# Rotation of the keys two products earlier in an in-order schedule (hybrid attention and gMLP block, one core)

## The chip, the cores and the metric

One NeuronCore of a Trainium2 chip runs the whole program. The metric is the device time of one execution in microseconds; the kernel before takes 1201.62 us (median of three runs, 1200.4 to 1201.99).

## The reference: what is computed

The block has 2048 tokens of width 1024. An RMS norm with a shift and a scale that come from a vector c gives h; one wide product gives all branches; attention (window of 128, 8 query heads, 2 key heads, a learned sink in each softmax) and a gated MLP that mixes over tokens in chunks of 128 are gated, projected, merged and projected again. What bears on the change is the rotation of q and k by the token's position:

```python
h = _rms(x, g_pre[l]) * (1.0 + scale) + shift
proj = h @ w_in[l]
q, k, v, z_a, u_b, v_b, z_b, g_logits = jnp.split(proj, SPLIT_IDX, axis=-1)
q = _rope(q.reshape(b, s, N_Q_HEADS, HEAD_DIM), positions)
k = _rope(k.reshape(b, s, N_KV_HEADS, HEAD_DIM), positions)

def _rope(t, positions):
    half = HEAD_DIM // 2
    inv_freq = ROPE_THETA ** (-jnp.arange(half, dtype=jnp.float32) / half)
    ang = positions.astype(jnp.float32)[..., None] * inv_freq
    cos = jnp.cos(ang)[:, :, None, :]
    sin = jnp.sin(ang)[:, :, None, :]
    t1, t2 = tf[..., :half], tf[..., half:]
    return concatenate([t1 * cos - t2 * sin, t2 * cos + t1 * sin], axis=-1)
```

## The kernel before, in words

**Tiles and products.** Tokens are handled in two halves of 1024 (`s` = 0, 1). The wide product is cut into 19 column groups of 256; each group is a 2 by 2 block product that is done with seven block products (numbered p = 0 to 6) instead of eight. One such product is 12 matmuls of 128x128 by 128x512: four slices of the inner dimension, three matmuls each, since every fp32 operand is split into a high and a low part (`mm3`, line 170). I call these "products" and number them as the program does with `slot`, from 0, along the first token half. The groups are: two of the MLP's v branch, the keys and values (`ev_kv`, line 983), one of gates, the first half of the queries (`ev_q`, line 1015), and so on. The first four groups are run side by side, so that products 0 to 27 belong to them, in turn: the key group's quarter for tokens 0 to 511 (call it k0) comes out of product 14, its quarter for tokens 512 to 1023 (k1) out of product 22. From product 28 on the groups follow one another, seven products each: 28 to 34 are the first queries, 35 to 41 a gate group, 42 to 48 the other queries.

**An order written out by hand.** Every engine executes its instructions strictly in the order in which the program issues them. Side work is hung on products: `later(n, f)` puts f ahead of the product n places on; with `True` behind it, with `"mid"` in its middle (after two of the four inner slices). Hooks of one place run in the order in which they were registered. An instruction hung on product 33 is therefore not at the time of product 33: it comes when its engine has done all that was issued earlier. This holds for the DMA queue of SyncE (SP) too: all loads and stores named here are issued by SP, in this order, and a transfer whose source isn't ready holds up all behind it.

**Weights.** `w_get` ahead of product n prepares the weight of product n + 3: SP loads `raw`, GpSimd (POOL) forms a sum of quarters where needed, ScalarE (ACT) casts the high part (line 223), and VectorE (DVE) subtracts for the low part ahead of the next product (lines 158 and 224). There are four weight buffers, so the cast for product n + 3 waits until product n - 1 is done.

**The rotation.** `rope_out` (line 639) turns the angles into a sine and a cosine table on ACT and stores both to DRAM (`cs`). `load_rope` (line 861) loads from there four tables, sine and cosine for each 512 tokens (`ropet`, buffers `m`), each by four DMAs of 64 KB; three products after a sine table's load ACT flips the sign of half its rows (line 870). `rope_finish` (line 947) has five steps, at 1, 5, 6, 8 and 9 products plus `wait` after the quarter came out: `turn` loads the quarter (`R`) and a copy with rows exchanged in pairs (two DMAs); `mix` multiplies the copy by the sine on POOL (line 961) and `R` by the cosine on DVE (line 962); `both` adds them on DVE and casts the high part on ACT; `low` subtracts on DVE; `put_out` stores high and low part (`k_s`). In the first token half the raw keys are kept in DRAM (`kr`) until then, so that a `turn` for them is three DMAs.

**What lies around it.** Ahead of or behind the same products hang: `setup_sgu` (product 26: loads of `wT` and `Tt`), `zero_heads` (28), `ln_step` (line 920) of the MLP branch, whose first three loads `q<-vb` (line 923) hang on products 27, 29 and 32, and whose transposes on TensorE (line 929) come behind products 31, 33 and 36 and wait for those loads; `h1_stats` (line 1189; product 30, then each fifth), which loads a row block of x and squares it on ACT three products on. A quarter that comes out of product p = 4 of a group is finished by an addition on DVE, `add(c, b["Y"], self.wsb)` (lines 436 and 164), and product p = 6 of that group, which accumulates in the same bank Y, waits until DVE has read it. In the gate group of products 35 to 41 these are product 39 and product 41.

Of the kernel before, what the change touches and what calls it, by code (L numbers as in the profile page):

```python
# [55 lines left out]
def hybrid_block(ctx: ExitStack, tc: tile.TileContext, xt, x, wada, wgate, wI, wP, wO,  # L56
# [30 lines left out]
    def flat(tag, dt=F32):  # L87
        return t2(tag, [P, 512], dt)
# [10 lines left out]
    def dram(name, shape):  # L99
        return tc.dram_tile(shape, F32, name=name)  # L100
# [16 lines left out]
    kr_s = [dram(f"kr{i}", [P, TG]) for i in range(2)]  # L117
# [39 lines left out]
    def sub(o, a, b):  # L157
        dve.tensor_tensor(out=o, in0=a, in1=b, op=ALU.subtract)  # L158

    def psub(o, a, b, op=ALU.subtract):  # L160
        pool.tensor_tensor(out=o, in0=a, in1=b, op=op)  # L161

    def add(o, a, b):
        dve.tensor_tensor(out=o, in0=a, in1=b, op=ALU.add)  # L164
# [64 lines left out]
    def later(n, f, post=False):  # L229
        hooks.setdefault((slot[0] + n, post), []).append(f)  # L230
# [630 lines left out]
    def load_rope(s, ns):  # L861

        def one(h, i, key):
            g = 2 * s + h
            t = flat("m")
            for r in range(4):
                at = 64 * (r // 2) + r % 2
                sp.dma_start(t[at : at + 64 : 2, :] if at < 64 else t[at:P:2, :], cs_s[i][32 * g : 32 * (g + 1), :])
            if key == "s":
                later(3, lambda: act.activation(out=t, in_=t, func=AF.Copy, scale=col[:, C_SGN : C_SGN + 1]))  # L870
            ropet[key, h] = t
        for h in range(2):
            for i, key in enumerate("cs"):
                later(ns[2 * h + i], lambda h=h, i=i, key=key: one(h, i, key))
# [29 lines left out]
    def half(key):  # L904
        return int(key[1]) - 1

    def ft(key):
        return int(key[0]) - 1

    def store(n, dst, t):  # L910
        later(n, lambda: sp.dma_start(dst, t))
# [35 lines left out]
    def rope_finish(h, R, put_out, wait, raw=None):  # L947
        st = {}

        def turn():  # L950
            nonlocal R
            if raw is not None:
                R = flat("x")
                sp.dma_start(R, raw)
            st["hi"] = flat("x", F32R)
            st["rot"] = st["hi"].bitcast(F32)
            for r in range(2):
                sp.dma_start(st["rot"][r:P:2, :], (R if raw is None else raw)[1 - r : P : 2, :])

        def mix():  # L960
            psub(st["rot"], st["rot"], ropet["s", h], ALU.mult)
            dve.tensor_tensor(out=R, in0=R, in1=ropet["c", h], op=ALU.mult)

        def both():
            add(R, R, st["rot"])
            act.copy(st["hi"], R)

        def low():
            sub(R, R, st["rot"])
        later(1 + wait, turn)  # L970
        later(5 + wait, mix)
        later(6 + wait, both, True)
        later(8 + wait, low)
        later(9 + wait, lambda: put_out(st["rot"], R))

    def rope_in(src, psum, tag):
        if not psum:
            return src
        R = flat(tag)
        act.copy(R, src)  # L980
        return R

    def ev_kv(s):
        def ev(key, src, psum):
            h = half(key)
            if ft(key) == 0:
                def put_out(hi, lo):
                    ks = slice(P + s * NT + h * 512, P + s * NT + (h + 1) * 512)
                    for i, t in enumerate((hi, lo)):
                        sp.dma_start(k_s[:, i, ks], t)  # L990
                R = rope_in(src, psum, "e")
                if s == 0:
                    store(1, kr_s[h], R)
                rope_finish(h, R, put_out, (15, 9)[h] if s == 0 else h, kr_s[h] if s == 0 else None)
            else:
                t = src
                if psum:
                    t = flat("e")
                    act.copy(t, src)

                def turn():
                    b = bank()
                    for c in range(4):
                        pe.transpose(b[:, c * P : (c + 1) * P], t[:, c * P : (c + 1) * P], ident)

                    def out_():
                        o = flat("qS"[s])
                        act.copy(o, b)
                        at = 1 + s * 8 + h * 4
                        store(1, v_s[:, at : at + 4, :], o.rearrange("p (a b) -> p a b", a=4))  # L1010
                    later(1, out_)
                later((3, 10)[h] if s == 0 else 2, turn, True)
        return ev
# [309 lines left out]
    def run_all():  # L1323
        nonlocal T

        for s in range(NS):
# [6 lines left out]
            if s == 0:  # L1333
                later(26, setup_sgu)
                later(28, zero_heads)
            load_rope(s, ((29, 28, 31, 30), (10, 11, 12, 13))[s])
            for i in range(8):
                later((27 + 5 * i // 2, 17 + 3 * i)[s], lambda i=i: ln_step(s, i))
            for c in range(4):
# [25 lines left out]
            if s == 0:  # L1365
                n0 = NFIRST
                S = pS.tile([P, 2, 512], F32, tag="s", name=nm("s"))
                bX = bank()
                rows["bank"] = bank()
                bks = [two_banks(BK["X"], BK["W"]), two_banks(BK["Y"], BK["Z"]), two_banks(S[:, 0, :], S[:, 1, :]),  # L1370
                       two_banks(bX, rows["bank"])]
                blks = [Block(bks[i], kinds[i](), "mmee"[i]) for i in range(NFIRST)]

                def second_root():
                    sum_to(NFIRST + 1)
                    rstd(1, BK["Z"])

                def second_half():
                    ada_row(1, range(0, 1))
                    want(NFIRST)  # L1380
                    want(NFIRST + 1)
                    sum_to(NFIRST + 3)
                    low_now()
                    sum_to(NFIRST + 4)
                    rope_do(1)
                    rstd_out(1, BK["W"])
                    ada_row(1, range(1, 4))
                    t_y(1, 0)
                    for kt in range(4):
                        t_d(1, kt)  # L1390
                        t_hi(1, kt)
                        if kt < 3:
                            t_y(1, kt + 1)
                        t_lo(1, kt)
                    want(NFIRST + 3)
                    low_now()

                def second_rows():
                    sum_to(2 * NFIRST + 2)
                    ada_fin(1)  # L1400
                    for kt in range(4):
                        t_y(2, kt)
                        t_d(2, kt)
                        t_hi(2, kt)

                def fetch_all():
                    cur["cap"] = 1 << 30
                later(NFIRST - 1, second_root, "mid")
                later(NFIRST - 1, second_half, True)
                later(NFIRST, lambda: ada_row(1, range(4, 6)), "k0")  # L1410
                later(NFIRST, lambda: ada_row(1, range(6, 8)), "mid")
                later(NFIRST, lambda: ada_rows_out(1), "mid")
                later(NFIRST + 1, second_rows, "mid")
                for kt in range(4):
                    later(NFIRST + 2 + kt // 2, lambda kt=kt: t_lo(2, kt), True)
                later(2 * NFIRST, fetch_all, True)
                later(NFIRST, lambda: sp.dma_start(mcpt, mcp))
                later(NFIRST, lambda: sp.dma_start(snk8, sinks.broadcast_to([P, 8])))
                for i in range(9):
                    later(9 + i, lambda: rope_do(1), True)  # L1420
                later(26, rope_out, "mid")
                later(12, lambda: dve.tensor_scalar(out=snk8, in0=snk8, scalar1=1.0 / SM, scalar2=None, op0=ALU.mult))
                for p in range(3, 7):
                    for i, (n, post) in enumerate(((-4, True), (-3, False), (-3, True), (-2, False), (-2, True), (-1, False))):
                        later(NFIRST * p + n, lambda p=p, i=i: t_part(p, i), post)
                for p in range(7):
                    lo = 0
                    if p in (0, 2):
                        lo = 2
                        ws = [w_get(), w_get(LA - 1)]  # L1430
                        step(lambda: high_first(blks, p, ws, T, p == 2))
                        step(lambda: None)
                    for i in range(lo, NFIRST):
                        w = w_get()
                        step(lambda: blks[i].run(p, w, T))
# [207 lines left out]
```

## Time and profile before

| what | value |
|---|---|
| median of three runs | 1201.62 us (1200.4 to 1201.99) |
| the profiled execution: its own time | 1203.53 us |
| its span, first to last instruction | 1201.8 us |
| mean granted TensorE clock in the span | 0.997 |
| busy: TensorE, weight load, DVE, ACT, POOL | 1184.4, 945.6, 869.2, 644.0, 342.4 us |
| DMA, mean rate | 260 GB/s |

The profiled execution's own time is 1.9 us above the median of the others. Times below are microseconds from the start of the span. In a timeline row the first number is the start, the second the duration of the instruction or of the merged group (with its count after x), and square brackets tell the idle time before it and who ended it. Matmuls are pipelined, so that their rows overlap a little. A suffix q marks an engine's sequencer; all of SP's rows are such, and the rows of its DMA issues tell how long the issue took, not the transfer.

### The profile page before, as it was taken

The numbers are of one execution on the slowest core, as the hardware profiler recorded it, in microseconds if no ns is written. First come the engines' busy times: TensorE is split into PE (matmuls) and PEld (weight loads), VectorE is DVE, ScalarE is ACT, GpSimd is POOL, SyncE is SP. The second block draws the span as 40 slices with busy tenths as digits, with TensorE's granted clock in tenths as the row PEclk, the third lists the DMA queues.
The fourth block names the chain that finished last, engine by engine and source line by source line (L and its number), as shares of the span: only waits on it lengthen the run. The fifth ranks groups of instructions, "written<-read, shape, count | busy, mean of one in ns | idle before, by whom it ended". The sixth has DMA issues, their size and how long they took to land.

```text
span 1201.8 us, 17373 instructions
## 1 busy us (share of the span) xinstructions
PE 1184.4 (99%) x5440; PEld 945.6 (79%) x5440; DVE 869.2 (72%) x1320; ACT 644.0 (54%) x1379; POOL 342.4 (28%) x290
## 2 busy tenths in 40 slices
PE   8999999999999999999999999999999999999997
PEld 4677878888777777888888887777778878888886
DVE  6897688678876676355866886554877977767775
ACT  5476455568765685443444766555845412444443
POOL 0001455333365201112201113130042301255453
PEclk9999999999999999999999999999999999999999
DMA  9546898959899997868779998998968987846352
GB/s 354 232 150 205 268 358 316 279 162 296 258 329 347 310 318 271 279 221 263 254 233 278 269 292 244 317 306 254 330 199 287 383 262 261 290 149 191 129 179 88
DMA packets 228548, 312.78 MB, mean 260 GB/s; under 512 B 20964, under 2 KB 103012, under 8 KB 228456
## 3 DMA queue, kind: packets, MB, share of 16 engines
q1 hardware_dynamic: 227984, 310.99, 79.5%
q8 instruction: 43, 0.70, 0.2%
q14 instruction: 49, 0.40, 0.1%
q0 software_dynamic: 176, 0.53, 0.1%
q10 hardware_dynamic: 296, 0.16, 0.1%
HBM read 201.82 MB, written 105.06 MB: 255 GB/s over the span
## 4 chain that ended last, share of the span: by engine, by line
PE 83%; DVE 6%; DMA 5%; ACT 2%; issue 2%; SPq 1%; POOL 0%; ACTq 0%; DVEq 0%; POOLq 0%
PE bankY L175 27%; PE bankX L175 19%; PE bankW L175 11%; PE bankZ L175 11%; PE b L175 3%; PE s L175 2%; PE b L1168 2%; PE s L1118 1%; PE s L1119 1%; DMA raw<-in_wP 1%; PE b L1057 1%; DVE W L158 1%; PE b L1153 1%; DMA raw<-sS 1%; DVE e L164 1%
## 5 line engine op out<-in xcount | busy, mean ns | idle before, releaser
L175 PE MATMUL bankY<-T,W 128*128 128x512 f32 x1566 | 383.2, 393 | 2.6 <-DVE e L164 2.3
L175 PEld LDWEIGHTS bankY<-T,W 128*128 128x128 f32 x1566 | 291.7, 188 | 64.3 <-issue 3.7
L158 DVE TENSOR_TENSOR W<-raw,W 128x512 fp32r<-128x512 f32 x327 | 268.5, 827 | 73.4 <-ACT W L223 70.5
L223 ACT CAST W<-raw 128x512 fp32r<-128x512 f32 x327 | 201.8, 618 | 131.0 <-PE b L175 41.9
L175 PE MATMUL bankX<-T,W 128*128 128x512 f32 x1098 | 266.9, 391 | 0.1
L175 PEld LDWEIGHTS bankX<-T,W 128*128 128x128 f32 x1098 | 204.2, 188 | 41.9 <-DVE T L803 0.5
L175 PE MATMUL bankW<-T,W 128*128 128x512 f32 x672 | 165.7, 393 | 2.9 <-DVE T L158 2.0
L175 PE MATMUL bankZ<-T,W 128*128 128x512 f32 x672 | 163.8, 391 | 0.0
L175 PEld LDWEIGHTS bankW<-T,W 128*128 128x128 f32 x672 | 124.4, 188 | 32.7 <-DVE T L158 3.5
L175 PEld LDWEIGHTS bankZ<-T,W 128*128 128x128 f32 x672 | 124.9, 188 | 27.2 <-ACT T L392 1.6
L161 POOL TENSOR_TENSOR S<-x,x 128x512 f32<-128x512 f32 x28 | 37.1, 1329 | 239.1 <-DMA x<-yb 107.8
L161 POOL TENSOR_TENSOR raw<-raw,raw 128x512 f32<-128x512 f32 x46 | 73.9, 1606 | 93.1 <-DVE W L158 44.3
L161 POOL TENSOR_TENSOR S<-raw,raw 128x512 f32<-128x512 f32 x23 | 34.9, 1518 | 168.8 <-DMA raw<-in_wI 74.5
L158 DVE TENSOR_TENSOR T<-x,T 128x512 fp32r<-128x512 f32 (+1 forms) x105 | 73.6, 748 | 3.6 <-ACT T L392 3.6
L164 DVE TENSOR_TENSOR e<-bankY,e 128x512 f32<-128x512 f32 x43 | 29.7, 690 | 59.2 <-PE bankY L175 59.0
L175 PE MATMUL b<-T,W 128*128 128x512 f32 x282 | 69.7, 390 | 0.5 <-DVE W L158 0.5
L175 PEld LDWEIGHTS b<-T,W 128*128 128x128 f32 x282 | 52.8, 188 | 11.8 <-DVE W L158 0.9
L175 PE MATMUL s<-T,W 128*128 128x512 f32 x246 | 60.1, 389 | 0.2 <-DVE e L164 0.2
L392 ACT CAST T<-x 128x512 fp32r<-128x512 f32 x100 | 56.0, 619 | 3.8 <-PE s L175 2.1
L175 PEld LDWEIGHTS s<-T,W 128*128 128x128 f32 x246 | 46.1, 188 | 10.2 <-issue 0.6
L161 POOL TENSOR_TENSOR raw<-S,raw 128x512 f32<-128x512 f32 x23 | 32.7, 1424 | 70.1 <-DVE W L158 58.5
L1147 ACT ACTIVATE P<-P,rc 128x128 f32<-128x128 f32 x128 | 44.5, 396 | 11.6 <-DVE rc L1143 11.6
(292 smaller groups left out, 1459.0 us busy)
## 6 DMA issues: line engine op xcount, KB each, us to landing
raw<-in_wI SPq DMA_DIRECT2D x127, 256.0 KB, 4.6
raw<-sS SPq DMA_DIRECT2D x92, 256.0 KB, 5.0
g<-e SPq DMA_DIRECT2D x64, 256.0 KB, 4.1
sS<-raw SPq DMA_DIRECT2D x43, 256.0 KB, 4.4
T<-in_wada SPq DMA_DIRECT2D x16, 512.0 KB, 8.2
q<-q SPq DMA_DIRECT2D x64, 128.0 KB, 5.4
q<-k_s SPq DMA_DIRECT2D x64, 128.0 KB, 4.9
raw<-m SPq DMA_DIRECT2D x32, 256.0 KB, 4.1
```

What stands on the lines that cost most here:

```text
L158: dve.tensor_tensor(out=o, in0=a, in1=b, op=ALU.subtract)
L161: pool.tensor_tensor(out=o, in0=a, in1=b, op=op)
L164: dve.tensor_tensor(out=o, in0=a, in1=b, op=ALU.add)
L175: pe.matmul(o, w[:, i, sl], t[:, j, kt, :], start=start and kt == kts[0] and n == 0, stop=stop and kt == last and n == 2, skip_group_check ...
L223: act.copy(w[:, 0, :], src)
L392: act.copy(T[p][:, 0, kt, :], rs[kt])
L1057: pe.matmul(b[:, ch * P : (ch + 1) * P], st["v", h][:, ch, :], wT[:, c, :], start=True, stop=True)
L1118: pe.matmul(o, q[:, g, :], k[:, 0, :], start=True, stop=False)
L1119: pe.matmul(o, q[:, g, :], k[:, 1, :], start=False, stop=True)
L1147: act.activation(out=st["P", kv][:, g, 0:P], in_=st["P", kv][:, g, 0:P], func=AF.Copy, scale=st["rc", kv][:, g : g + 1])
L1153: pe.transpose(t[:, g * P : (g + 1) * P], st["P", kv][:, g, 0:P], ident)
L1168: pe.matmul(o[own, :], v[:, k, own], st["pv", kv][k], start=k == 1, stop=k == 0)
```

## The change

Three hook distances in the first token half become smaller by two. The stores of the sine and cosine tables move from the middle of product 26 to the middle of product 24. The four table loads move: sine and cosine for tokens 0 to 511 from products 28 and 29 to 26 and 27, those for tokens 512 to 1023 from 30 and 31 to 28 and 29; the sign flips on ACT go with them, from 31 and 33 to 29 and 31. And the five steps of the keys' rotation move: for k0 from products 30, 34, 35, 37 and 38 to 28, 32, 33, 35 and 36, for k1 from 32, 36, 37, 39 and 40 to 30, 34, 35, 37 and 38. Nothing is added or taken away, and the rotation of the queries, the second token half and all other hooks stay where they are.

```diff
@@ ev_kv, the keys' rotation @@
                 if s == 0:
                     store(1, kr_s[h], R)
-                rope_finish(h, R, put_out, (15, 9)[h] if s == 0 else h, kr_s[h] if s == 0 else None)
+                rope_finish(h, R, put_out, (13, 7)[h] if s == 0 else h, kr_s[h] if s == 0 else None)
@@ run_all, table loads (cos, sin of tokens 0-511, then cos, sin of 512-1023) @@
-            load_rope(s, ((29, 28, 31, 30), (10, 11, 12, 13))[s])
+            load_rope(s, ((27, 26, 29, 28), (10, 11, 12, 13))[s])
@@ run_all, the two Sin activations and the stores of their tables @@
-                later(26, rope_out, "mid")
+                later(24, rope_out, "mid")
```

## The prediction

> **What bounds the kernel now.** I read the page first, for the engines' shares; then what TensorE waits for; then the granted clock in stretches around the one large wait; then the timelines of TensorE, DVE, ACT and SP from 105 to 165 us, the stretch in which the moved work lies.
>
> ```profile
> PE 1184.4 (99%) x5440; PEld 945.6 (79%) x5440; DVE 869.2 (72%) x1320; ACT 644.0 (54%) x1379; POOL 342.4 (28%) x290
> ```
>
> ```profile
> PE bankY L701 <- DVE T L700: 3.5, 1, 3.5
> PE bankY L175 <- DVE e L164: 2.3, 1, 2.3
> ```
>
> TensorE is busy for 99% of the span, the change removes no matmul, and apart from the start (3.5 us, ahead of everything that moves) one wait alone is over a microsecond: 2.3 us for a DVE addition. Only what that wait costs can be gained. In stretches of 3.41 us:
>
> ```profile
> 106.13:109.54 3.41, 2.34 (x9) 1.27 (x8) 3.41 (x7) 1.14 (x2) 0.00 (x0) 1.00 0.20 77
> ...
> 157.33:160.74 3.41, 1.18 (x5) 1.04 (x6) 3.38 (x7) 1.29 (x3) 1.73 (x3) 1.00 1.05 366
> 160.74:164.15 3.41, 3.41 (x10) 2.55 (x10) 3.41 (x5) 0.92 (x2) 2.78 (x3) 0.50 1.00 341
> ```
>
> After the stretch's length the columns are busy TensorE, weight load, DVE, ACT and POOL, then granted clock, DMA share and GB/s. TensorE idles 2.23 us of 157.33 to 160.74, and in the 3.41 us after it the clock is 0.50. An idle 1.07 us of 106.13 to 109.54 had no such effect. TensorE's timeline:
>
> ```profile
> 117.95 2.89 PE L175 MATMUL bankX<-T,W 128*128 128x512 f32 x12
> ...
> 130.69 0.60 PE L929 MATMUL b<-cst,q 128*128 128x128 f32 x4
> ...
> 133.89 2.89 PE L175 MATMUL bankZ<-T,W 128*128 128x512 f32 x12
> 136.61 0.60 PE L929 MATMUL b<-cst,q 128*128 128x128 f32 x4
> ...
> 145.24 0.60 PE L929 MATMUL b<-cst,q 128*128 128x128 f32 x4
> ...
> 159.56 4.44 PE L175 MATMUL bankY<-T,W 128*128 128x512 f32 x12 [2.34 <-DVE e L164]
> ```
>
> The rows are products 28 and 33, the transposes behind products 31, 33 and 36, which matter below, and product 41. The wait (157.22 to 159.56) is ahead of product 41, whose 12 matmuls then take 4.44, until 164.00, against the 2.72 that product 33 has to itself (136.61 less 133.89): 1.72 us more. **The whole stall costs 2.34 + 1.72 = 4.06 us**, the most that can be won. DVE is late because it works without a pause:
>
> ```profile
> 139.73 0.69 DVE L933 BATCH_NORM_STATS2 bst<-b 128x6 f32<-128x512 f32 x1
> ...
> 141.95 0.81 DVE L941 TENSOR_SCALAR q<-b,mv,rv 128x512 f32<-128x512 f32 x1 [0.74 <-POOL rv L155]
> 142.67 0.68 DVE L164 TENSOR_TENSOR x<-x,x 128x512 f32<-128x512 f32 x1
> 143.27 0.69 DVE L158 TENSOR_TENSOR W<-raw,W 128x512 fp32r<-128x512 f32 x1
> 143.87 0.69 DVE L962 TENSOR_TENSOR x<-x,m 128x512 f32<-128x512 f32 x1
> 145.08 1.17 DVE L962 TENSOR_TENSOR x<-x,m 128x512 f32<-128x512 f32 x1 [0.52 <-DMA x<-x]
> 146.18 1.78 DVE L158 TENSOR_TENSOR W<-raw,W 128x512 fp32r<-128x512 f32 x1
> ...
> 158.76 0.66 DVE L164 TENSOR_TENSOR e<-bankY,e 128x512 f32<-128x512 f32 x1
> ```
>
> From the statistics behind product 33's transposes (139.73) to the addition (158.76) DVE needs 19.03 us with 1.26 us of idle (0.74 and 0.52), for hooks that include the rotations of k0, k1 and the first queries.
>
> **The change part by part.** *ACT.* The two Sins move ahead of the Gelu of product 24's result.
>
> ```profile
> 110.33 0.60 ACT L223 CAST W<-raw 128x512 fp32r<-128x512 f32 x1
> 110.83 0.59 ACT L916 ACTIVATE e<-bankW 128x512 f32<-128x512 f32 x1
> ...
> 113.83 1.28 ACT L643 ACT_TABLE_LOAD   x1
> 115.13 0.63 ACT L643 ACTIVATE m<-m 128x512 f32<-128x512 f32 x1
> 115.67 0.71 ACT L645 ACTIVATE m<-m,col 128x512 f32<-128x512 f32 x1
> ...
> 117.38 1.28 ACT L1044 ACT_TABLE_LOAD   x1
> ```
>
> Now: table load 1.28, Sin, Sin, and another load for the Tanh at 117.38. After: the load at 110.94, Sins ending at 112.87 and 113.49 (the offsets of the rows: 115.13 + 0.63 and 115.67 + 0.71, less 113.83), a load for the Gelu to 114.8, the Gelu to 115.4, where it ended at 111.42. Still two loads: nothing is added on ACT. The cast for product 28 comes behind that Gelu, at 115.3 to 115.9, its low part on DVE ends near 116.6, and product 28 starts at 117.95; later casts have more to spare. On TensorE's path: 0, with a cover of 1.3 us. The Trainium skill ("ScalarE: Activation LUTs", What ACT_TABLE_LOAD costs) gives a switch 1283 ns plus a drain of some 1380 ns. The rows show the Sin 1.30 us after its load's start and no drain; by the page's figure the Gelu would end 2.8 us later still, and so would all that follows from it.
>
> *SP* is what I take for decisive, since 18 table DMAs, six loads and four stores of the keys move ahead of others on it.
>
> ```profile
> 111.45 0.32 SPq L911 DMA_DIRECT2D vb<-e  x1
> 111.82 0.42 SPq L877 DMA_DIRECT2D wT<-in_ws  x1
> 112.34 0.41 SPq L878 DMA_DIRECT2D Tt<-in_bs  x1
> 113.34 0.33 SPq L911 DMA_DIRECT2D vb<-e  x1
> 115.79 0.93 SPq L646 DMA_DIRECT2D cs<-m  x2
> 116.77 0.42 SPq L246 DMA_DIRECT2D raw<-in_wI  x1
> ...
> 122.46 2.42 SPq L868 DMA_DIRECT2D m<-cs  x4
> ...
> 128.45 0.59 SPq L923 DMA_DIRECT2D q<-vb  x1
> ...
> 139.90 0.64 SPq L954 DMA_DIRECT2D x<-kr  x1
> ```
>
> From the row at 116.77 to that at 139.90 SP issues 37 DMAs almost without a pause: 23.13 / 37 = 0.62 each (four `m<-cs` take 2.42). It lags behind the products: the `turn` of k1, hung on product 32 (131.0, by the transposes ahead of it), is issued at 139.90. Moving hooks two products (5.4 us) earlier thus can't make their DMAs that much earlier; they only push others back. New order: `vb` waits for the Gelu until 115.4, so the queue begins its unbroken run there. Then 33 issues, counted in the order of hooks, stand before the second `q<-vb` (product 29): vb, wT, Tt, 4 m, vb, raw, 4 m, the first q<-vb, 2 sS, 2 raw, k_s, v_s, 4 m, 3 kr, sS, g, 4 m. 33 x 0.62 = 20.5, less some 0.9 since the first are cheap (0.32 to 0.42 in their rows): issue at **135.0 instead of 128.45**. The times from issue to landing, from the DMA view of 116.7 to 141.8 (count, KB each, then median us):
>
> ```profile
> m<-cs SPq DMA_DIRECT2D x16, 64.0 KB, 2.4
> q<-vb SPq DMA_DIRECT2D x3, 256.0 KB, 3.4
> ...
> x<-kr SPq DMA_DIRECT2D x2, 256.0 KB, 3.1
> ```
>
> I take 3.1 (the row whose DMAs were issued nearest to 135), ends 2.4 and 3.4, and for the 33 issues one microsecond either way: landing at 138.1, from 136.4 to 139.4. TensorE's transposes behind product 33 are due at 136.61, and all behind them on TensorE waits: **a new wait of 1.5 us, from 0 to 2.8**. The first `q<-vb` (issue 122.6) lands before 126.5, its transposes come at 130.69: 0. The third is issued near 140.8 and lands at 143.9, with TensorE at 145.24: 0. The weight loads that slip (some 4 to 6 us) are cast three products ahead of use: 0; if that cover were gone each late microsecond would be one of TensorE.
>
> *DVE and POOL.* `mix` of k0 now stands ahead of the statistics of product 32, and its loads, issued from 129.8 on, land from 132.9: DVE, in order, stands 1.5 us there, and the addition for product 34 ends near 136.2, ahead of the transposes that precede that product: 0. `mix` of k1 needs a load that comes four issues behind the second `q<-vb`: 137.5, landing 140.6. Statistics behind product 33's transposes thus at 141.2 instead of 139.73, 1.5 later. From there to the addition: 19.03, less `both` of k0 and `mix` of k1 (pitch 0.60 each, now ahead of it), less the 1.26 of idle, whose causes then lie before: 16.6. POOL's multiplications stay in that stretch, all six, so long DVE rows such as that of 146.18 (1.78 against 0.68) stay too. Addition from 157.8 to 158.5, ends 1.1 us either way (one such long row more or less). Moving the four k_s stores and the sign flips: 0, since nobody reads k_s before product 60; the flips hold ACT at product 31 until the sine lands, some 4 us, beneath the three products of the weights' lead.
>
> *The sum.* Product 41 could start at 157.22 + 1.5 = 158.7 by TensorE and at 158.6 by DVE: 158.7 instead of 159.56, **0.8 us gained** (bounds: 0.8 later to 2.3 sooner). The clock: 1.5 us idle in one place lies between the 1.07 that cost nothing and the 2.23 that cost 1.72; nearer to 1.07, and it may fall on two stretches, so I take 0 for the loss: another 1.72 gained in this execution, 2.5 in all. The Trainium skill ("TensorE: Matmul & The Clock Gate", Part 1) says that the clock halves after at least one idle window of about 3.4 us, which runs freely. The length agrees with the 3.413 seen here, but 2.34 us of idle had already brought it down; by the page no wait of the new kernel under 3.4 us would halve the clock.
>
> The sum stands against this execution's own 1203.53. The runs shown spread from 1200.4 to 1201.99, about the size of that clock loss, so that I take half of it as already missing in the median: 1201.62 - 0.8 - 0.8 = **1200.0 us**. Under 0.2% (2.4 us) either way is about what a measurement of this kernel can't tell from no change.
>
> **The rivals.**
> *The stall simply goes* (0.30). SP runs 1.5 us ahead of my count, the second `q<-vb` lands by 136.6, and DVE ends its addition by 157.2. Then 2.34 to 4.06 us are gained: 1197.6 to 1199.3. For it: `m<-cs` land in 2.4, and DVE idled before the stretch. Against it: the 0.62 per issue.
> *The new wait grows beyond the old one* (0.12, slower). The second `q<-vb` lands as late as the worst of its line:
>
> ```profile
> DMA to landing us min/median/max: 2.9/3.9/6.4
> ```
>
> This is from the view of line 923 over the whole span (16 loads). At 135.0 + 6.4 = 141.4 TensorE would wait 4.8 at product 33 and lose 1.72 to the clock: product 41 from 163.7 to 166.5 instead of to 164.0, 2.5 later, **1204.1**; SP late by another microsecond, 1205.1. It decides from a landing of 141.3 on. Against it: the median of the three loads of this stretch is 3.4.
> (With the drain of the page on ScalarE, 2.8 later than 138.1, the landing would be 140.9 and the time some 1203.6.)
> *It does nothing* is a part of my forecast: two waits share what one had, and only the clock differs.
>
> **How the numbers follow.** Forecast 0.58 (its own range 1199.2 to 1202.5), stall gone 0.30, wait grown 0.12. Faster by over 0.2% (below 1199.2): 0.30 and a little of the forecast, 0.33. Slower (above 1204.0): 0.10. The rest, 0.57, is within. The range 1197.6 to 1203.8 reaches to the full gain and almost to the third case.
>
> **What would show it.** SP's first `vb` store at 115.4 and the second `q<-vb` issued at 135 (if under 133, my count of the queue is wrong); a wait of TensorE ahead of the transposes at 136.6 for DMA q<-vb; DVE's k1 `mix` waiting for x<-kr until 140.6; the addition of product 39 near 158; no granted clock of 0.5 in mid-span. Wrong it would be if TensorE waited nowhere there, or if the addition came after 159.5 and its wait stayed beside the new one.

## The result, and the profile after

The changed kernel took 1205.22 us in the median, beside 1201.33 us for the kernel before on the same chip: a ratio of 1.0028, 95% interval [1.0018, 1.0038]. It is slower by 3.9 us. Measured twice more on other occasions it was 1.0018 [1.0007, 1.0029] and 1.0018 [1.0010, 1.0027], so 2 to 4 us is its size. The forecast was 1200.0 us with a range to 1203.8.

The profiled execution after took 1205.35 us, with a span of 1203.6. The page's line of the engines' busy time:

```profile
PE 1182.6 (98%) x5440; PEld 944.2 (78%) x5440; DVE 865.9 (72%) x1320; ACT 645.8 (54%) x1380; POOL 350.0 (29%) x290
```

No engine has noticeably more to do than before: POOL's 290 instructions take 7.6 us longer, and ACT has one instruction more, a table load that comes up again below. What changed is who waits. The waits of TensorE between 130 and 165 us (line waited at, releaser, then us in total, times and the longest):

```profile
PE b L929 <- DMA q<-vb: 2.3, 1, 2.3
PE bankY L175 <- DVE e L164: 1.7, 1, 1.7
```

Where before had one wait of 2.3 us there are two of 2.3 and 1.7. The first is the forecast's new wait, at the transposes behind product 33. The second is the old one, ahead of product 41, and it has not gone. The timeline shows both chains, first the queue SP:

```profile
115.33 0.32 SPq L911 DMA_DIRECT2D vb<-e  x1
...
135.86 0.60 SPq L923 DMA_DIRECT2D q<-vb  x1
...
138.12 0.43 SPq L954 DMA_DIRECT2D x<-kr  x1
```

and then DVE and TensorE:

```profile
133.38 0.69 DVE L962 TENSOR_TENSOR x<-x,m 128x512 f32<-128x512 f32 x1 [4.33 <-DMA x<-kr]
...
138.96 0.63 PE L929 MATMUL b<-cst,q 128*128 128x128 f32 x4 [2.28 <-DMA q<-vb]
...
142.59 0.69 DVE L962 TENSOR_TENSOR x<-x,m 128x512 f32<-128x512 f32 x1 [2.15 <-DMA x<-kr]
143.20 0.69 DVE L933 BATCH_NORM_STATS2 bst<-b 128x6 f32<-128x512 f32 x1
...
146.15 0.81 DVE L941 TENSOR_SCALAR q<-b,mv,rv 128x512 f32<-128x512 f32 x1 [0.46 <-POOL rv L155]
...
154.61 0.81 DVE L941 TENSOR_SCALAR q<-b,mv,rv 128x512 f32<-128x512 f32 x1 [0.44 <-POOL rv L155]
...
160.53 0.66 DVE L164 TENSOR_TENSOR e<-bankY,e 128x512 f32<-128x512 f32 x1
161.33 2.99 PE L175 MATMUL bankY<-T,W 128*128 128x512 f32 x12 [1.72 <-DVE e L164]
```

DVE stands 4.33 us for the first half of k and 2.15 us for the second. From the second half's `mix` on it works through almost without a pause and comes to the addition of product 39 at 160.53, where before it came at 158.76. Product 41 starts at 161.33 instead of 159.56: 1.77 us later, and TensorE has no slack behind it. In this execution the clock stays full in mid-span, while in the profile of before it was halved behind product 41, so that TensorE is only 0.3 us late at the end of product 41 (164.32 against 164.00). The two spans differ by 1.8 us. The other 1.5 us arise far from the change: by the starts of the same matmuls, the changed kernel loses 3.1 us between 690 and 750 us, where TensorE has these waits:

```profile
PE s L1118 <- DMA q<-k_s: 1.2, 1, 1.2
PE bankY L175 <- DVE W L158: 0.5, 1, 0.5
PE bankY L175 <- ACT bankY L445: 0.5, 2, 0.3
```

The kernel before loses 1.6 us near 951 and 963 us instead, with two waits of 0.2 and 0.9. Two later profiles of the same changed kernel (after_again and after_third) have no wait of TensorE above 0.2 us behind 172 us and are nonetheless 2.6 and 2.3 us longer in span than a repeated profile of before (before_again). In both the delay is there early: transposes that start at 168.28 in before_again start at 171.68 and 171.12. So the late waits are a matter of the single execution, and 161 us is where to look.

### The profile page after: what moved, and what is told of

The parts are those of the page before. It is cut to its first block, busy times and chain, and to the rows that moved or that the text cites. A ratio compares the mean times of both kernels' runs of the same rounds, so it can differ in the third digit from the quotient of the medians.

```text
span 1203.6 us, 17377 instructions
## 1 busy us (share of the span) xinstructions
PE 1182.6 (98%) x5440; PEld 944.2 (78%) x5440; DVE 865.9 (72%) x1320; ACT 645.8 (54%) x1380; POOL 350.0 (29%) x290
## 4 chain that ended last, share of the span: by engine, by line
PE 79%; DVE 8%; DMA 5%; ACT 3%; issue 2%; SPq 1%; POOL 0%; ACTq 0%; DVEq 0%; POOLq 0%
PE bankY L175 26%; PE bankX L175 18%; PE bankW L175 11%; PE bankZ L175 10%; PE b L175 4%; PE s L175 3%; PE b L1168 2%; DVE W L158 2%; PE s L1118 1%; PE s L1119 1%; PE b L1153 1%; PE b L1057 1%; DVE e L1029 1%; DMA e<-za 1%; ACT W L223 1%
## 5 line engine op out<-in xcount | busy, mean ns | idle before, releaser
L158 DVE TENSOR_TENSOR T<-x,T 128x512 fp32r<-128x512 f32 (+1 forms) x105 | 69.2, 708 | 2.8 <-ACT T L392 2.8
```

## The experiments

Each was run beside the kernel before on the same chip. Here are all of them at a glance; the last three columns, in us, are from each one's profile: what TensorE waited at product 33's transposes, when DVE began the addition of product 39, and when product 41 started.

| kernel | median (before) | ratio, 95% interval | wait at 33 | addition | product 41 |
|---|---|---|---|---|---|
| before_again | 1202.44 (1202.06) | 1.0001 [0.9992, 1.0010] | none | 158.70 | 159.50 |
| tables_only | 1205.40 (1202.06) | 1.0028 [1.0017, 1.0038] | 0.22 | 160.65 | 161.45 |
| rotation_only | 1204.84 (1202.06) | 1.0021 [1.0011, 1.0030] | none | 160.57 | 161.37 |
| early_ln | 1205.21 (1202.06) | 1.0031 [1.0019, 1.0043] | 0.71 | 160.76 | 161.56 |
| after_again | 1203.87 (1201.93) | 1.0018 [1.0007, 1.0029] | 3.03 | 162.12 | 162.93 |
| two_after | 1202.61 (1201.93) | 1.0005 [0.9996, 1.0015] | 2.37 | 159.68 | 161.08 |
| two_before | 1201.85 (1201.93) | 0.9998 [0.9988, 1.0007] | none | 159.01 | 159.82 |
| k0_only | 1203.37 (1201.93) | 1.0010 [1.0002, 1.0019] | 2.15 | 160.31 | 161.11 |
| before_fill | 1200.97 (1201.87) | 0.9990 [0.9979, 1.0001] | none | 158.37 | 159.18 |
| after_fill | 1204.04 (1201.87) | 1.0016 [1.0004, 1.0028] | 0.72 | 161.77 | 162.58 |
| k1_later | 1200.58 (1201.87) | 0.9986 [0.9977, 0.9996] | none | 155.30 | 157.38 |
| after_third | 1203.94 (1201.84) | 1.0018 [1.0010, 1.0027] | 3.23 | 161.58 | 162.38 |
| after_fill_again | 1203.65 (1201.84) | 1.0018 [1.0009, 1.0027] | 1.24 | 162.25 | 163.06 |
| after_k1_later | 1204.91 (1201.84) | 1.0023 [1.0011, 1.0034] | 3.73 | 160.45 | 162.97 |
| k1_later_again | 1200.87 (1201.84) | 0.9988 [0.9979, 0.9997] | none | 156.74 | 157.55 |
| both_away | 1202.43 (1202.03) | 1.0001 [0.9991, 1.0010] | 0.49 | 158.40 | 159.20 |
| before_fill_again | 1201.05 (1202.03) | 0.9994 [0.9985, 1.0002] | none | 157.03 | 158.31 |

### The two halves of the change, and the wait at product 33 taken away

before_again is the kernel before, unchanged. tables_only is before with the second and third line of the change (the tables two products sooner), rotation_only with its first line (the steps of the keys' rotation). early_ln is the changed kernel with the second `q<-vb` issued ahead of the second sine table's loads (product 28) instead of behind the second cosine table's (product 29), its transposes, statistics and normalization staying where they were:

```diff
-    def ln_step(s, i):
+    def ln_step(s, i, d=0):
...
-        later(4, turn, True)
-        later(5, stats)
-        later(6, norm)
+        later(4 + d, turn, True)
+        later(5 + d, stats)
+        later(6 + d, norm)
...
+            if s == 0:
+                later(28, lambda: ln_step(0, 1, 1))
             load_rope(s, ((27, 26, 29, 28), (10, 11, 12, 13))[s])
-            for i in range(8):
+            for i in [i for i in range(8) if (s, i) != (0, 1)]:
```

> The kernel before, unchanged, as a control: ratio 1.000, and a second profile of it. Local theory (the change costs what it delays product 41's start, from 159.56 to 161.33 us, because VectorE's addition of product 39 is late): product 41 again at 159.6 +/- 0.3; the half clock behind it may be there or not, since the stretches in which the clock is judged begin at another time in each run. Late-stall theory (the change's cost lies in TensorE's waits between 690 and 750 us, where the changed kernel's profile lost 3.0 us and that of before nothing): no wait over 0.3 us there in this kernel. Chance theory (those waits come and go by run in either kernel): some of them here too.

> Only the Sines and the four table loads two products sooner; the keys' rotation as before. Local theory: the second q<-vb load is issued three issues sooner than in the changed kernel (134.1 instead of 135.9) and lands at 137, wait at product 33 0.3 to 0.8 us; the keys' loads about as before, product 41 at 159.0 to 159.8, time within 1 us of before. Theory that the wait at product 33 is itself the cost: +0.5 us. Late-stall theory, if the moved tables set it off: +3 us.

> Only the five steps of the keys' rotation two products sooner; Sines and tables as before. Local theory: the second q<-vb load is issued at 130.2, no wait at product 33; VectorE's multiplication for the second key quarter now waits for its cosine table (issued last, landing near 142), product 41 at 160.5 to 161.5, time 1 to 2 us over before. Theory that the wait at product 33 is the cost: no slower than before, -1 to 0 us. Late-stall theory, if the rotation's place sets it off: +3 us.

> The changed kernel with one load moved: the second q<-vb is issued ahead of the four sine loads of product 28 instead of behind the cosine loads of product 29 (its transposes, statistics and normalisation stay where they were). Theory that the wait at product 33 is the cost: that wait (2.28 us) goes and the time falls by 2 us or more, to that of before or below. Local theory: the wait goes, but VectorE still waits for the second key quarter until 142.5 and adds at 160.5, so that TensorE waits 4 us ahead of product 41 instead of 1.7; product 41 at 161.0 to 161.6, time as the changed kernel within 1 us.

The control agrees with itself. Each half of the change alone costs as much as the whole, by a different way. In tables_only the keys' loads stand behind the tables in the queue and land later, and DVE begins the first `mix` at 140.54 (138.02 before):

```profile
140.54 0.69 DVE L962 TENSOR_TENSOR x<-x,m 128x512 f32<-128x512 f32 x1 [2.48 <-DMA S<-in_x]
145.78 2.39 DVE L962 TENSOR_TENSOR x<-x,m 128x512 f32<-128x512 f32 x2
160.65 0.66 DVE L164 TENSOR_TENSOR e<-bankY,e 128x512 f32<-128x512 f32 x1
```

(The releaser named is the latest of several that this instruction waits for; the same keys had landed at 140.47.) I had expected at most 1 us from the tables; that was wrong. In rotation_only the keys are there and the tables are not:

```profile
132.92 0.69 DVE L962 TENSOR_TENSOR x<-x,m 128x512 f32<-128x512 f32 x1 [3.07 <-DMA m<-cs]
...
143.05 0.69 DVE L962 TENSOR_TENSOR x<-x,m 128x512 f32<-128x512 f32 x1 [3.62 <-DMA m<-cs]
...
160.57 0.66 DVE L164 TENSOR_TENSOR e<-bankY,e 128x512 f32<-128x512 f32 x1
```

There is no wait at product 33 in it, and yet product 41 starts at 161.37. And early_ln, which takes most of that wait away from the changed kernel, gains nothing: the wait ahead of product 41 grows to 2.79 instead. So the wait that the forecast thought decisive isn't what sets product 41; DVE is.

### Fewer issues on the queue, and the first half of k alone

two_after and two_before store each table's rows twice, so that a table comes back in two loads of 64 rows in place of four of 32:

```diff
-    cs_s = [dram(f"cs{i}", [P, TG]) for i in range(2)]
+    cs_s = [dram(f"cs{i}", [2 * P, TG]) for i in range(2)]
...
-            sp.dma_start(cs_s[i], t)
+            for a in range(2):
+                sp.dma_start(cs_s[i][a : 2 * P : 2, :], t)
...
-            for r in range(4):
-                at = 64 * (r // 2) + r % 2
-                sp.dma_start(t[at : at + 64 : 2, :] if at < 64 else t[at:P:2, :], cs_s[i][32 * g : 32 * (g + 1), :])
+            for r in range(2):
+                sp.dma_start(t[64 * r : 64 * (r + 1), :], cs_s[i][64 * g : 64 * (g + 1), :])
```

k0_only is the changed kernel with the second half of k as before:

```diff
-                rope_finish(h, R, put_out, (13, 7)[h] if s == 0 else h, kr_s[h] if s == 0 else None)
+                rope_finish(h, R, put_out, (13, 9)[h] if s == 0 else h, kr_s[h] if s == 0 else None)
```

> The changed kernel, unchanged: a second profile, and its times beside those of the others of this job. Queue theory (SP's queue is late, VectorE stands at the second key quarter's multiplication until its load has landed, and with it the addition of product 39 is late): multiplication again near 142.5, addition near 160.5, product 41 near 161.3, and the half clock behind product 33 or 41 in most runs; 3 to 4 us over before. Late-stall theory: waits of 2 to 3 us in all between 690 and 750 us again; chance theory: under 1 us there.

> The changed kernel with half as many table loads: each table is stored with every row doubled (two stores instead of one), so that a load is two DMAs of 64 contiguous rows instead of four of 32; the bytes loaded are the same, SP issues 6 DMAs fewer. Queue theory: the second q<-vb is issued near 132.2 and lands by 135.5 (no wait at product 33); the second key quarter lands near 138, its multiplication near 138.7, addition of product 39 near 156.6 to 157.5, product 41 at 157.2 to 158.2 with a wait under 1 us and no half clock: 2 to 4 us below before. Rival, the bytes in flight and not the issues hold the loads up: landings as in the changed kernel, product 41 at 161, 3 us over before.

> The kernel before with half as many table loads (as in the kernel of the same kind), the hooks where they were. Queue theory: SP comes 3.7 us earlier to the loads behind product 30, VectorE loses its 0.5 us of waiting for x<-x and little else, since there its own work sets the pace from 139.7 on: product 41 at 158.7 to 159.3, 0.3 to 1.5 us below before. Rival: no change.

> The changed kernel with the second key quarter's rotation put back (products 32 to 40 again); Sines, tables and the first quarter stay two products sooner. Queue theory: the wait at product 33 for q<-vb stays (about 2.2 us), but VectorE no longer stands behind it: statistics near 139.5, addition of product 39 near 158, product 41 at 159.3 to 159.8, set by the wait at 33: within 1 us of before. If instead VectorE stands at another rotation load: 160.5 or later, 2 to 3 us over before.

With fewer issues the changed kernel comes within what can be told from before, while the same edit does nothing for before. In two_after's trace SP issues the second `q<-vb` 1.2 us sooner (134.65), but it takes 4.19 us to land in place of 2.96, so the wait at 33 is the old one. What did come sooner is the second half of the keys, issued at 136.90 and landed at 141.62:

```profile
141.65 0.69 DVE L962 TENSOR_TENSOR x<-x,m 128x512 f32<-128x512 f32 x1 [0.75 <-DMA x<-kr]
...
159.68 0.66 DVE L164 TENSOR_TENSOR e<-bankY,e 128x512 f32<-128x512 f32 x1
```

Here a rule can be read off. From the second `mix` to the addition it is 18.03 us; in the changed kernel's three profiles 160.53 - 142.59 = 17.94, 162.12 - 144.12 = 18.00 and 161.58 - 143.61 = 17.97; in early_ln 17.93, in the two runs below that fill waits in the changed kernel (after_fill, after_fill_again) 17.92 and 17.97. TensorE's own waits differ by 3 us among these and leave the distance alone. (In rotation_only, where that `mix` waits for its table and not for its keys, it is 17.52.) The addition is the second half's `mix` plus 18 us, and the `mix` is the landing of its load.

In two_after the addition alone doesn't set product 41, though. TensorE starts it at 161.08 without a wait for DVE, because it comes late itself: it had waited 2.37 us at product 33 and ran the next 3.41 us at half clock.

In k0_only that half is later, so DVE should be free; it comes to the addition at 160.31 all the same, because another engine stands for the queue. ACT waits for the row block of x that `h1_stats` squares, the casts of the weights stand behind it in ACT's order, and DVE waits for a cast:

```profile
141.88 0.63 ACT L1193 ACTIVATE S<-S 128x512 f32<-128x512 f32 x1 [7.19 <-DMA S<-in_x]
```

```profile
144.33 0.69 DVE L158 TENSOR_TENSOR W<-raw,W 128x512 fp32r<-128x512 f32 x1 [3.44 <-ACT W L223]
```

### How much of it is the half clock

before_fill puts two products of the constant ones into the wait ahead of product 41, so that TensorE doesn't idle; nobody reads their result. after_fill does the same with two ahead of product 33's transposes and one ahead of product 41:

```diff
+    def fill(n):
+        f = pS.tile([P, 2, 512], F32, tag="s", name=nm("s"))
+        for _ in range(n):
+            pe.matmul(f[:, 0, :], ones, wide, start=True, stop=True, skip_group_check=True)
...
+            if s == 0:
+                later(33, lambda: fill(2), True)
+                later(41, lambda: fill(1))
```

> Before, with two 128x512 products of the constant ones (by the rows of the opening of the kernel 0.85 us each) put on TensorE between product 40 and product 41, into a bank that nobody reads; they lie in a wait that was 2.34, 1.90 and 2.33 us in three profiles of before's order. If the half clock that follows this wait (3.41 us at 0.5 in one profile of before, none in two others) is drawn by the idle time, it is gone in every run: product 41 still starts near 159.5, and the median falls by the 1.7 us times its share of the runs, some 0.3 to 1.0 us (1201.0 to 1201.6 beside 1202). If the half clock does not hang on the wait, nothing changes (within 0.2 us).

> After, with two such products ahead of product 33's transposes (wait 2.28 and 3.03 us in two profiles) and one ahead of product 41 (wait 1.72 and 1.28 us). The starts of the transposes and of product 41 do not move (138.9 to 139.4, 161.3 to 162.9). Theory, shift plus half clock: of after's loss of 2 to 3.5 us against before the half clock holds 1 to 1.7 us and the later start of product 41 the rest, so the time falls to 1202.7 to 1203.9 beside 1202 for before, still slower. Rival, the half clock is the whole loss: it falls to before's time or under. Rival, the half clock plays no part: it stays at 1204 to 1205.2.

> After unchanged, so that after_fill_again is compared with it on the same chip. The two comparisons so far gave 1.0028 and 1.0018 of before; expected 1.0018 to 1.0028 again, 1203.9 to 1205.2 beside 1201.9.

> After with the three products of constants as before (two ahead of product 33's transposes, one ahead of product 41). If the half clock is a part of after's loss in most runs, it is 0.8 to 1.7 us below after_third and still 1.3 to 2.2 us above before. If the loss is the later start of product 41 alone, the two differ by under 0.5 us.

> Before with two products of constants in the wait ahead of product 41, as it was. The first comparison gave 0.9990 [0.9979, 1.0001] of before. Expected 0.9986 to 0.9994 if the half clock follows before's wait in about half of its runs; 0.9997 to 1.0003 if the first was chance.

No stretch of mid-span is at 0.5 in these four fill profiles. The kernel before gains 0.9 and 1.0 us in the median, at the upper end of what I expected, though both intervals still reach 1: that its own median holds about half of a half-clock loss is likely, not shown (in before_fill_again DVE also came to the addition 1.3 us sooner). The changed kernel gains 0.3 us against itself on the same chip, which is nothing. The trace of after_third says why. Its stretches, with the columns as in the prediction (length, TensorE, weight load, DVE, ACT, POOL, granted clock, DMA share, GB/s):

```profile
137.09:140.50 3.41, 0.82 (x6) 0.80 (x7) 3.41 (x6) 0.00 (x0) 1.35 (x2) 1.00 0.86 229
140.50:143.92 3.42, 3.42 (x10) 2.64 (x9) 0.32 (x2) 1.90 (x6) 0.00 (x0) 0.50 1.01 369
```

After the 3.23 us wait at product 33 the clock is halved from 140.50 on. But this lies ahead of the wait for DVE's addition, and takes its place:

```profile
PE b L929 <- DMA q<-vb: 3.2, 1, 3.2
PE bankY L175 <- DVE e L164: 0.4, 1, 0.4
```

TensorE arrives at product 41 late and waits 0.45; in after_fill_again it arrives in time at full clock and waits 1.84. The start is DVE's in both. A half clock ahead of a wait for another engine costs nothing as long as that wait outlasts it; in two_after and, below, in after_k1_later none is left, and TensorE itself is late. One behind the wait, as in tables_only, early_ln and rotation_only, costs time: the rows of product 41 take 4.56, 4.39 and 5.46 us instead of some 3.0 (in rotation_only two stretches, 6.83 us at 0.5).

### The second half of k later, and both limits taken away

k1_later goes the other way: in the kernel before, the second half's steps hang on products 36, 40, 41, 43 and 44.

```diff
-                rope_finish(h, R, put_out, (15, 9)[h] if s == 0 else h, kr_s[h] if s == 0 else None)
+                rope_finish(h, R, put_out, (15, 13)[h] if s == 0 else h, kr_s[h] if s == 0 else None)
```

after_k1_later is the changed kernel with `(13, 13)` in that place; both_away is after_k1_later with early_ln's edit. after_again and after_third are the changed kernel unchanged.

> Before, with the rotation of k's second half four products later instead of two sooner: reload at 36, mix and addition at 40 and 41, subtraction at 43; the tables stay. Theory, DVE's work in the stretch from 138 to 158.7 sets product 41: about 3.6 us of the rotation's work (mix 1.17, addition 0.69, subtraction 1.78) leaves the stretch, the addition of product 39 waits for its bank alone, ahead of 157.5, and product 41 starts within 0.5 us of product 40's end: 1.5 to 2.3 us gained there and no half clock, 1199.0 to 1200.5 beside 1202, unless the work is given back as a wait of TensorE between products 42 and 46 (then 1201 to 1202). Rival, the queue of SP and its landings set product 41: the addition stays at 158 to 159 and the time at before's.

> The version with k's second half four products later than in before, as it was. Expected 0.9980 to 0.9992 of before; the first comparison gave 0.9986 [0.9977, 0.9996].

> After, with k's second half not two products sooner than in before but four later (six later than in after); the tables and the first half stay sooner. Theory, the work of VectorE sets product 41, the queue of SP sets product 33's transposes: the wait ahead of product 41 is gone (under 0.5 us), the wait at product 33 stays (1.5 to 3 us), and since a wait of TensorE costs its length the kernel stands where before stands with its one wait of 1.9 to 2.3 us: 1201 to 1203 beside 1201.9. Rival, product 41 is late because TensorE, and so product 39, is late by the wait at product 33: product 41 stays at 161 or later, and the time at after's.

> After, with the second half-column read of the statistics ahead of the sine tables' loads (as in early_ln) and with k's second half at 36, 40, 41 and 43 instead of 30, 34, 35 and 37 (as in after_k1_later). Theory, two limits in series (SP's queue for the transposes of product 33, VectorE's work behind the second half's mix for product 41): neither is left, TensorE waits under 1 us at product 33 and under 0.5 us at product 41, no half clock, and the time is that of k1_later, 1200.0 to 1201.5 beside 1201.9 for before, 3 us under after. Rival, a third limit (the first half's mix waiting for tables or keys): product 41 stays at 161 or later and the time at 1203 to 1205.

k1_later beats both kernels: 0.9986 and 0.9988 of before, with intervals that end at 0.9996 and 0.9997. DVE has the second half's work behind it, comes to the addition before TensorE needs it, and product 41 starts without a wait:

```profile
155.30 0.66 DVE L164 TENSOR_TENSOR e<-bankY,e 128x512 f32<-128x512 f32 x1
```

```profile
157.38 2.89 PE L175 MATMUL bankY<-T,W 128*128 128x512 f32 x12
167.63 3.01 PE L175 MATMUL bankY<-T,W 128*128 128x512 f32 x12 [0.94 <-ACT bankY L445]
```

Of the 2.1 us that product 41 is sooner than in before_again, 0.9 is given back as a wait ahead of a product at 167.63. In k1_later_again two waits, of 0.88 and 1.02 us, give back nearly all: that product starts at 169.14, beside 168.75 in before_again, which has no half clock, and 170.26 in before, which has one. Filling before's wait had gained 0.9 and 1.0 us; k1_later gains 1.3 and 1.0. So its gain may be mostly the half clock that no longer follows, and not the earlier start; no run separates the two.

after_k1_later missed my expectation, and the rival that I had named for it holds. With DVE out of the way TensorE has no wait ahead of product 41, yet starts it at 162.97, because it had waited 3.73 us at product 33 and then ran 3.41 us at half clock. So there are two limits, one behind the other and nearly of one size: SP's queue for the transposes of product 33, and DVE for product 41. Taking either away (early_ln 1.0031, after_k1_later 1.0023) shows the other. Taking both away (both_away) brings product 41 to 159.20 and the time to 1.0001 of before:

```profile
PE bankY L175 <- ACT bankY L445: 1.0, 1, 1.0
PE bankW L175 <- DVE W L158: 0.7, 1, 0.7
PE b L929 <- PE bankZ L175: 0.5, 1, 0.5
PE bankY L175 <- DVE e L164: 0.5, 1, 0.5
```

These are TensorE's waits from 130 to 172 us: the two limits are down to 0.5. I had expected the time of k1_later, and it came to that of before. The waits of 0.7 and 1.0, at 166 and 170 us, don't explain this, since k1_later_again has them too. What differs lies ahead of them: DVE stands 5.49 us for the first half's keys, until 135.21, and comes to the addition that product 34 waits for at 137.66 instead of 134.50 in k1_later_again, so that product 34 starts at 138.49 instead of 137.38 and product 41 at 159.20 instead of 157.55. The first half's `mix` is thus a third limit, the rival that I had named, though smaller than I had put it.

## Why the prediction was wrong, point by point

- **ACT: right in this stretch.** The Sins run at 112.14 and 112.68, the Gelu ends at 115.30 (115.4 was said), and there are still two table loads here. That nothing is added on ACT is not so: behind the Gelu's load the Tanh needs none, but the first Exp at L1138, at 233.32, now needs a load of 1.28 us at 232.03 that before did not have. TensorE has no wait there. Each Sin or Gelu follows 1.29 us behind its load's start, without the drain that the Trainium skill ("ScalarE: Activation LUTs", What ACT_TABLE_LOAD costs) adds.

```profile
110.85 1.28 ACT L643 ACT_TABLE_LOAD   x1
112.14 0.63 ACT L643 ACTIVATE m<-m 128x512 f32<-128x512 f32 x1
112.68 0.71 ACT L645 ACTIVATE m<-m,col 128x512 f32<-128x512 f32 x1
113.41 1.28 ACT L916 ACT_TABLE_LOAD   x1
114.70 0.60 ACT L916 ACTIVATE e<-bankW 128x512 f32<-128x512 f32 x1
...
232.03 1.28 ACT L1138 ACT_TABLE_LOAD   x1
233.32 0.37 ACT L1138 ACTIVATE P<-s,nb 128x129 f32<-128x129 f32 x1
```

- **The queue and the new wait: the mechanism right, 0.8 to 1.7 us short.** The unbroken run begins at 115.33 as said, and 33 issues stand ahead of the second `q<-vb` as counted. They take 20.53 us, 0.62 each, so that the 0.9 us struck off for cheap first issues wasn't there: it is issued at 135.86, not 135.0, and lands 2.96 us later. The wait is 2.28 us against 1.5, inside the bounds of 0 to 2.8; the two other profiles of the same kernel, 3.03 and 3.23, lie outside them.
- **The landing of k1's keys: the term that failed.** 138.12 was the issue (137.5 said), but it landed 4.35 us later and not 3.1: DVE's second `mix` is at 142.59, where 140.6 was taken, and at 144.12 and 143.61 in the other two profiles. The 3.1 came from the loads of before. Between issue and landing of this one the DMA engines were 0.87 busy there and are 1.03 busy now (the last two columns are DMA share and GB/s; first before, then after):

```profile
139.90:143.03 3.13, 3.13 (x16) 2.58 (x15) 2.36 (x5) 1.37 (x3) 1.10 (x2) 1.00 0.87 283
```

```profile
138.12:142.47 4.35, 3.51 (x18) 3.00 (x19) 2.32 (x4) 1.36 (x5) 0.90 (x1) 1.00 1.03 354
```

  The same load took 3.77 us at a share of 0.93 (rotation_only), 4.47 at 1.03 (tables_only), 4.72 at 1.02 (two_after), and 5.60 and 4.97 at 1.01 and 1.00 in the other two profiles of the changed kernel; but it took 4.10 at only 0.78 in two_before. That the crowd of transfers makes the landing late fits most of these rows; no run changed the crowd alone, so why the landing is late stays open.

- **DVE's stretch: 0.75 us short.** From the second `mix` to the addition I had 0.6 + 16.6 = 17.2; it is 17.94. I had struck out all idle time, saying that its causes would lie before; two waits for POOL's `rv` remained, 0.46 and 0.44, the rows shown above. For the first half DVE stood 4.33 us, where I had 1.5; this did no harm, since the addition for product 34 still ended at 136.50 (136.2 said).
- **The sum.** 142.59 - 140.6 = 2.0 and 0.75 make 2.7: product 41 at 161.33 instead of the 158.6 that the forecast had by DVE. By TensorE's own path alone it would have started at 159.6 (161.33 less its wait of 1.72), where before stood, so the forecast's gain of 0.8 us was lost at product 33 already, and DVE added the rest. In the other two profiles product 41 starts at 162.93 and 162.38, 3.4 and 2.9 us later than in before_again, which is about the 2 to 4 us measured. The 1.1 us either way that I gave to DVE's end were for one long row; the landing that its whole stretch hangs on carried no bound of its own, though the neighbouring load of the same queue had one. And the tables' part was priced through its issues alone, while tables_only shows the cost of the whole change.
- **The clock: right in the first profile, in part by luck.** There was no 0.5 in mid-span, as forecast. But the forecast was for a wait of 1.5 us; the wait was 2.28, about as long as the 2.34 that had brought before's clock down, and it cost nothing because it fell on two stretches with 1.14 us idle in each, which the forecast had named only as possible. In the two other profiles, after waits of 3.03 and 3.23 us, there was a half stretch. The Trainium skill's rule ("TensorE: Matmul & The Clock Gate", Part 1: at least one idle window of about 3.4 us) would allow none of these, since no wait reached 3.4 us; the row at 137.09 shows TensorE idle for 2.59 of 3.41 us ahead of the halving. The price of 1.72 us was a little high, since it set a row with its overlap (4.44) against one without (2.72): from product 41 to the transposes behind it at 169.90, before falls 1.56 us behind before_again, which has no half clock (159.56 and 159.50, then 169.90 and 168.28). The 0.8 us that the forecast took for the clock in the median isn't refuted: no profile of the changed kernel has a half stretch behind product 41. The later start outweighs it.
- **The rivals.** The time is that of the one with a chance of 0.12, but not by its mechanism: the second `q<-vb` landed at 138.82, far from the 141.3 where it was to decide. The place was DVE's wait for the keys. The sign that I had named for being wrong, the addition after 159.5 with its wait beside the new one, is what the trace shows.

## What to carry to other kernels

Hanging a load and its consumer earlier doesn't bring the data earlier when an in-order queue already runs without a pause; it brings the in-order consumer to its wait earlier, and all work of that engine behind it waits too. Find the load on which the bound engine's next release hangs, and give its landing a range taken from a stretch where the DMA engines are as busy as they will be. When DVE is the one that is late, move its work behind the release, not ahead of it: here four products later was worth 0.13% (how much of it through the clock is open), and two products sooner cost 0.2 to 0.3%.

## What had not been expected of the hardware

- The granted clock changed only on a grid of 3.413 us in each execution (38, 44 or 45 such stretches from the first record to the halving), and the halving went by the idle share of one stretch of that grid, not by the length of a wait. TensorE's idle time in the stretch ahead of a halving was 2.12 us (after_k1_later), 2.17 (early_ln), 2.23 (before), 2.37 (tables_only, two_after), 2.59 (after_third, rotation_only) and 3.02 (after_again). Stretches with up to 1.93 us idle (two_before; 1.72 in the profile after, ahead of product 41) were followed by full clock. The grid is counted from the first stretch that the records give. In these profiles the limit lies between 57% and 62% of a stretch at full clock. A stretch at half clock is another matter: in rotation_only one with only 0.83 us idle was followed by a second at 0.5. Before's wait of 2.3 us stands near it, and where the grid falls decides: in two_before a wait as long (2.33 us) fell on two stretches and cost no clock, as did the changed kernel's wait of 2.28 us at product 33 in its first profile. From two_before and from after_k1_later:

```profile
156.01:159.43 3.42, 1.48 (x7) 0.90 (x5) 3.39 (x5) 0.00 (x0) 1.30 (x2) 1.00 1.05 367
159.43:162.84 3.41, 3.02 (x14) 2.52 (x15) 3.41 (x5) 1.74 (x3) 2.75 (x3) 1.00 1.00 359
```

```profile
138.76:142.17 3.41, 1.29 (x8) 1.20 (x9) 3.21 (x5) 0.00 (x0) 1.39 (x2) 1.00 1.01 314
142.17:145.58 3.41, 3.41 (x10) 2.63 (x9) 0.41 (x3) 2.36 (x6) 0.76 (x2) 0.50 1.05 377
```

- Time from issue to landing of one 256 KB load of the keys, in the same place of the same kernel, was 4.35, 5.60 and 4.97 us in three profiles, and product 41 moved with it (161.33, 162.93, 162.38).
